# Reordering the first loads of a two-layer decoder trunk: x's first block in two halves, the first weights on ACT's queue, g's row alone

## The chip, the cores and the metric

The kernel runs on one core of a Trainium2 chip. The metric is the device time of one execution, in microseconds; the median of three runs stands for a kernel. The core has five engines that run side by side, each working through its own instructions in the order of the program: TensorE (PE, with its weight loads listed as PEld), VectorE (DVE), ScalarE (ACT), GpSimd (POOL) and SyncE (SP). They wait for one another through semaphores. Transfers are issued from the queues of SP, ACT and POOL.

## The reference

Two layers of a hybrid decoder on x of 512 tokens by 1024 channels, in float32. What matters here is the start of the first layer:

```
def hybrid_layer(x, positions, norm_g, w_in, ...):
    h = rmsnorm(x, norm_g)
    p = h @ w_in                       # (512 x 1024) @ (1024 x 3488)
    (cq, ckv, kr, g_a, ...) = jnp.split(p, offs, axis=-1)
    q = (rmsnorm(cq, mla_q_norm_g) @ mla_w_uq)...
    ...                                # rope(q, positions), attention, conv, gating, block-sparse attention
    return y @ w_out
```

rope needs the cosine and sine of positions times a fixed row of frequencies; positions are integers, one for each token.

## The kernel before

All matrix products split each float32 operand into a high and a low part and add three products (high by high, low weights by high, high by low). The order of all instructions is set at build time by a small planner: class `Order` keeps a model clock for each engine and a heap of generators; each generator is a chain of work that yields until its model time is due, and an instruction is put down when the planner reaches it. The planner moves instructions only between places in the build; on the chip each engine runs its list from the first to the last.

The start goes like this. `start` (L2068) issues the load of the first block of x (128 channels, k = 0, all 512 tokens) on SP, then puts down six matmuls on a tile of ones (`o.fill`, tile `warm`), whose results nobody reads. One more small matmul at L2082 turns 12 rows of the tile `junk` into 12 columns of PSUM: four rows of positions (cast from integers to floats by POOL at L539) and eight rows of the gain g of the first RMSNorm (`norm_g`). DVE copies them to the tile `pg`, whose two parts are called `posf` and `gcol`. The two rows were loaded by two issues on ACT's queue (L537, L538).

`c_first` (L1761) is the first piece of the projection, 416 columns wide, with four accumulators `cq` for the four groups of 128 tokens. It starts with `x_transpose(0)` (L749): four transposes on PE of x's first block into tile `xT`. Then ACT writes the high part `hTh`, scaled by `gcol`, and DVE the low part `hTl`. For each k the three groups of four matmuls follow: `whi` by `hTh`, then the next block's four transposes, `wlo` by `hTh`, `whi` by `hTl`.

The weights of `c_first` come in units `c0` to `c3`, two blocks of k in each. `load_units` (L408) loads unit c0 in two halves on SP and puts the load of x's second block (`load_xk(1, 2)`) between them; `split_units` (L446) makes the high part of each half, by DVE for the first half of c0 and by ACT for the others of c0 to c3, and `low_half` the low part by DVE.

POOL meanwhile fills masks and constants, clears the tile `prow` and issues six small loads of gains into it (`load_rows`, L616 to L623). The rope tables (`rope_tables`, L551, tile `rope_scratch`) come next on POOL and need `posf`. From there on, PE is the engine that everything is arranged around, to the last matmul.

Of the kernel before, what the change touches and what calls it, by code (L numbers as in the profile page):

```python
# [13 lines left out]
I32 = mybir.dt.int32  # L14
AF = mybir.ActivationFunctionType
# [3 lines left out]
P = 128  # L19
S = 512  # L20
NT = S // P
D = 1024
KT = D // P
# [35 lines left out]
def dram(ap, offset, pattern):  # L59
    return bass.AP(tensor=ap.tensor, offset=ap.offset + offset, ap=pattern)  # L60
# [91 lines left out]
def run_now(gen):  # L152

    try:
        next(gen)
    except StopIteration as e:
        return [e.value]
# [64 lines left out]
def hybrid_trunk(ctx: ExitStack, tc: tile.TileContext, x, positions, norm_g, w_c, w_f, w_t, w_o, mla_q_norm_g,  # L222
                 mla_w_uq, mla_kv_norm_g, mla_w_ukv, mla_q_g, mla_k_nope_g, mla_k_rope_g, conv_w,
                 sg_ln_g, sg_ln_b, sg_w, sg_b, moba_q_g, moba_k_g, out):
    nc = tc.nc
    V, A, G, PE = nc.vector, nc.scalar, nc.gpsimd, nc.tensor
# [16 lines left out]
    o = Order()  # L243
# [46 lines left out]
            yield from ch.wait(low)  # L290
        yield from ch.pe(c, PE.matmul, dst, sl, mh, start=False, stop=last, **k)

    def dma(ch, nbytes, dst, src):

        o.clk["D"] = max(o.clk["D"], ch.t) + nbytes / 360.0
        nc.sync.dma_start(dst, src)
        ch.t = o.clk["D"] + 2000.0

    x1d = dr.tile([S, D], F32, name="x1d")
# [108 lines left out]
    def load_units():  # L408
        for u in order:
            ch = Chain(o)  # L410
            u.raw_slots = rawS
            if u.name in ("uq_0", "ukv_0"):
                u.raw_slots = hS
                u.raw = yield from hS.get(ch, f"raw_{u.name}")
            elif u.name[:-3] in SPROD and u.name[-3] == "1":
                u.raw_slots = hS
                u.raw = yield from hS.get(ch, f"raw_{u.name}")
            elif u.name in ("sq2_0", "sq3_0"):
                u.raw_slots = v4S
                u.raw = yield from v4S.get(ch, f"raw_{u.name}", [P, D], F32)  # L420
            elif u.name in ("c2_0", "c3_0") or u.name[:-3] in ZPROD and u.name[-3] == "1":
                u.raw_slots = tkS
                u.raw = (yield from tkS.get(ch, f"raw_{u.name}", 96)).rearrange("p a b c -> p (a b c)")
            else:
                u.raw = yield from rawS.get(ch, u.name)
            key = (int(u.name[-1]), u.name[:-3], ord(u.name[-3]) - 48)
            if key in tsum_ev:
                yield from ch.wait(tsum_ev[key])
            n = u.a * u.b
            if u.name == "c0_0":  # L430
                for i in range(2):
                    sl = slice(i * n // 2, (i + 1) * n // 2)
                    ch = Chain(o)
                    dma(ch, P * n * 2, u.raw[:, sl], u.src[:, sl])
                    o.set(u.landed[i], ch.t)
                    if i == 0:
                        load_xk(1, 2)
            else:
                dma(ch, P * n * 4, u.raw[:, :n], u.src)
                ch.t += LATE.get(u.name, 0.0)  # L440
            o.set(u.loaded, ch.t)
            for e in LOAD_HOOKS.pop(u.name, ()):
                e()
            yield o.now

    def split_units(i0, i1):  # L446
        for u in order[i0:i1]:
            ch = Chain(o)
            if u.name != "c0_0":
                yield from ch.wait(u.loaded)  # L450
            u.hi, u.lo = yield from u.slots.get(ch, u.name)
            n = u.a * u.b
            gain = {"uq": 2 * int(u.name[-1]), "ukv": 4 + int(u.name[-1])}.get(u.name[:-2])
            if gain is not None:
                yield from ch.wait(pc_ev)
            for i in range(2):
                if u.name == "c0_0":
                    yield from ch.wait(u.landed[i])
                while ch.t > o.now + SLACK:
                    yield ch.t - SLACK  # L460
                while not u.wanted and max(o.clk["A"], o.clk["V"]) > o.now + WSLACK:
                    yield o.now + 100.0
                sl = slice(i * n // 2, (i + 1) * n // 2)
                c2 = Chain(o, max(o.now, ch.t))
                hi, lo, raw = u.hi[:, sl], u.lo[:, sl], u.raw[:, sl]
                g = None
                if gain is not None:
                    c = gain + (i if u.a == 2 else 0)
                    g = pcol[:, c:c + 1]
                if o.clk["V"] + 900.0 < o.clk["A"] and u.idx > 3 or u.idx == 0 and i == 0:  # L470
                    if g is None:
                        yield from c2.dve_fast(V.tensor_copy, hi, raw)
                    else:
                        yield from c2.dve(V.tensor_scalar, hi, raw, g, None, op0=ALU.mult)
                else:
                    yield from c2.act(A.activation, hi, raw, AF.Copy, scale=1.0 if g is None else g)
                o.set(u.high[i], c2.t)
                o.spawn(low_half(u, i, c2, lo, raw, hi, g), None, LOPRIO if u.idx < 4 else 5)
                ch.t = max(ch.t, c2.t - LAT)
# [54 lines left out]
    pg = cst.tile([P, NT + KT], F32, name="pg")  # L534
    posf, gcol = pg[:, 0:NT], pg[:, NT:]
    inv = cst.tile([P, 16], F32, name="inv")
    nc.scalar.dma_start(junk[0:NT, 0:P].bitcast(I32), dram(positions, 0, [[P, NT], [1, P]]))  # L537
    nc.scalar.dma_start(junk[NT:NT + KT, P:2 * P], dram(norm_g, 0, [[P, KT], [1, P]]))  # L538
    G.tensor_copy(junk[0:NT, P:2 * P], junk[0:NT, 0:P].bitcast(I32))  # L539
    for i in range(16):  # L540
        G.memset(inv[:, i:i + 1], THETA ** (-i * 2.0 / 32))
    one_box = run_now(zzS.get(Chain(o), "ones", F32R))
# [68 lines left out]

    pcol = cst.tile([P, 14], F32, name="pcol")
    pc_ev = Event()
    prow = []

    def load_rows():  # L616
        pr = prow[0]
# [123 lines left out]
    def load_xk(k0, k1):  # L741
        ch = Chain(o)
        c0 = (k0 % 2) * P
        src = x[0, :, k0 * P:k1 * P].rearrange("(t p) c -> p t c", p=P)
        dma(ch, P * NT * P * 4 * (k1 - k0), xk[k0 // 2][:, :, c0:c0 + (k1 - k0) * P], src)
        for k in range(k0, k1):
            o.set(xk_ev[k], ch.t)

# [995 lines left out]
    def main():  # L1744
# [16 lines left out]
        def c_first(L):  # L1761

            home = [accS, accS, accS, sS]
            a, us = [], {}
            for t in range(NT):
                a.append((yield from home[t].get(m, f"cq{t}_0")))

            def part(k, t, i):
                (hh, hl), (wh, wl) = hk(L, k), us[k]
                sl = slice(t * P, (t + 1) * P)  # L1770
                yield from m.pe(cost(416), PE.matmul, a[t][:, 0:416], (hl if i == 2 else hh)[:, sl],
                                wl if i == 1 else wh, start=k == 0 and i == 0, stop=k == KT - 1 and i == 2)

            def ready(k, i):
                u = units[f"c{k // 2}_0"]
                for v in order[u.idx:u.idx + AHEAD]:
                    v.wanted = True
                yield from m.wait((xhi[k], u.half[k % 2], xlo[k])[i])
                if i == 0:
                    yield from m.wait(u.high[k % 2])  # L1780
                    us[k] = [z[:, k % 2, :] for z in u.view()]

            yield from x_transpose(0)
            for k in range(KSPLIT):
                for i in range(3):
                    yield from ready(k, i)
                    for t in range(NT):
                        yield from part(k, t, i)
                    if i == 0 or i == 1 and k + 1 == KSPLIT:
                        yield from x_transpose(k + 1 + i)  # L1790
                    yield o.now
                if k % 2 == 1:
                    done_unit(f"c{k // 2}_0")
            for t, k in ((0, 6), (1, 6), (0, 7), (1, 7), (2, 6), (2, 7), (3, 6), (3, 7)):
                for i in range(3):
                    if t == 0:
                        yield from ready(k, i)
                    yield from part(k, t, i)
                yield o.now
                if k == KT - 1:  # L1800
                    o.spawn(low_chain(L, t, a[t], o.now + PELAT, home[t]))
            for k in range(KSPLIT // 2, KT // 2):
                done_unit(f"c{k}_0")
# [264 lines left out]
    def start():  # L2068
        o.clk["D"] = 1000.0
        cw = Chain(o)  # L2070
# [4 lines left out]
        ones = one_box[0][:, 0:P].bitcast(F32)  # L2075
        V.memset(ones, 1.0)
        V.tensor_copy(one_box[0][:, P:2 * P], ones)
        A.activation(xsum[:, 0, 0:1], ones[:, 0:1], AF.Square, scale=D ** -0.5)
        o.fill = lambda: PE.matmul(wp[:, 0:P], ones, ones, start=True, stop=True)
        for _ in range(NWARM):  # L2080
            o.fill()
        PE.transpose(wp[:, 256:256 + NT + KT], junk[0:NT + KT, P:2 * P], ident[0:NT + KT, 0:NT + KT])  # L2082
        V.tensor_copy(pg, wp[:, 256:256 + NT + KT])
        o.pe_end, o.fill_until = 3700.0, FILLEND
        o.clk["V"] = 3700.0

# [6 lines left out]
        LOAD_HOOKS["c0_0"] = (lambda: load_xk(2, 4),)  # L2093
        LOAD_HOOKS["c1_0"] = (lambda: load_xk(4, 6),)
        LOAD_HOOKS["c2_0"] = (lambda: load_xk(6, 8),)
        prow.append((yield from t2S.get(cw, "prow")))
        G.memset(prow[0][0:14, 0:P], 1.0)
        load_rows()
        o.clk["G"] = 10000.0
# [65 lines left out]
```

## Time and profile before

| what | value |
|---|---|
| median of three runs | 486.28 us (484.81 to 486.62) |
| profiled execution, span from first to last instruction | 484.2 us |
| profiled execution, time outside its span | not listed; the three runs lie 0.6 to 2.4 us above the span |
| PE busy | 478.2 us, 99% of the span |
| DVE, ACT, POOL busy | 399.4, 335.0, 115.2 us |
| first matmul of the projection (`cq`) starts at | 5.77 us |
| last matmul ends at about | 480.3 us |

The span is the time from the first to the last instruction of one profiled execution. A busy time adds the spans of an engine's instructions. Matmul ends are modelled, so consecutive matmuls overlap in the listing, and the distance of their starts is the better measure of pace.

### The profile page before, as it was taken

The page shows a single profiled execution, that of the slowest core. Times are in us where ns is not written, and L with a number is a line of the kernel's source. Part 1 is how long each engine was busy: PE and PEld are TensorE (multiplying, and loading weights), DVE is VectorE, ACT ScalarE, POOL GpSimd, SP SyncE. Part 2 cuts the span into 40 slices and gives each one's busy share as a digit, 9 for nine tenths or more (in the row PEclk, how much of TensorE's full clock was granted, in tenths as well). Part 3 has the DMA queues.
Part 4 walks back from the last instruction along what each step waited for, and adds up shares of the span by engine and source line. Part 5 has one row for each costly group of instructions (what it writes and reads, how often), then busy time and mean ns, then how long its engine had stood idle before and what let it go on. Part 6 is the DMA issues. An engine that isn't in the chain of part 4 may idle for free. (4 is left out here: it accounts for less than half of the span.)

```text
span 484.2 us, 7554 instructions
## 1 busy us (share of the span) xinstructions
PE 478.2 (99%) x2418; PEld 406.6 (84%) x2418; DVE 399.4 (82%) x883; ACT 335.0 (69%) x895; POOL 115.2 (24%) x187
## 2 busy tenths in 40 slices
PE   8999999999999999999999999999999999999996
PEld 7988888888888888888899888888888888888785
DVE  3698877978798997779898679997788998888992
ACT  5897757776568674457577788788686888676640
POOL 8858713310421052000031004262102200000000
PEclk9999999999999999999999999999999999999999
DMA  8823076996698798685663277987824852248762
GB/s 265 306 87 110 12 229 242 235 232 168 184 282 190 219 270 260 233 283 178 214 238 131 86 268 244 263 176 226 185 87 144 161 156 106 104 158 276 271 216 87
DMA packets 41760, 94.21 MB, mean 195 GB/s; under 512 B 6114, under 2 KB 22328, under 8 KB 41336
## 3 DMA queue, kind: packets, MB, share of 16 engines
q1 hardware_dynamic: 28400, 80.74, 48.2%
q0 software_dynamic: 13216, 12.91, 17.6%
q8 instruction: 19, 0.31, 0.3%
q14 instruction: 21, 0.17, 0.1%
q10 hardware_dynamic: 104, 0.07, 0.1%
HBM read 85.58 MB, written 33.29 MB: 246 GB/s over the span
## 5 line engine op out<-in xcount | busy, mean ns | idle before, releaser
L179 ACT ACTIVATE pd<-pd,mnd 128x128 f32<-128x128 f32 (+3 forms) x53 | 27.2, 541 | 3.7 <-DVE mnd L179 3.5
L179 ACT ACTIVATE pa<-pa,mna 128x128 f32<-128x128 f32 (+3 forms) x55 | 28.1, 539 | 1.8 <-DVE mna L179 1.6
L375 POOL DMA_DIRECT2D t<-in_w_o_dram x16 | 18.6, 1323 | 30.5 <-DMA t<-t 30.4
L179 ACT ACTIVATE pha<-pTa 128x512 fp32r<-128x512 f32 (+3 forms) x32 | 13.8, 436 | 15.1 <-PE pTa L209 14.5
L179 ACT ACTIVATE phd<-pTd 128x512 fp32r<-128x512 f32 (+3 forms) x32 | 13.7, 433 | 13.0 <-PE pTd L209 12.8
L209 PE MATMUL cq<-whi_c,hTh 128*128 128x416 f32 x64 | 20.6, 367 | 0.4 <-ACT hTh L179 0.3
L179 DVE TENSOR_TENSOR pla<-pTa,pha 128x512 fp32r<-128x512 f32 (+3 forms) x32 | 15.1, 485 | 7.1 <-ACT pha L179 7.0
L179 ACT ACTIVATE whi_t<-raw_t 128x512 fp32r<-128x512 f32 x32 | 18.5, 618 | 3.3 <-DMA raw_t<-t 3.3
L179 DVE CUSTOM_DVE_ANT_0 pa<-sa,maskb,rs_q 128x512 f32<-128x512 f32 (+3 forms) x32 | 16.6, 545 | 4.8 <-PE pTa L209 2.7
L179 DVE TENSOR_TENSOR wlo_t<-raw_t,whi_t 128x512 fp32r<-128x512 f32 x32 | 20.6, 680 | 0.0
L209 PE MATMUL cq<-wlo_c,hTh 128*128 128x416 f32 x64 | 20.0, 358 | 0.0
L209 PE MATMUL cq<-whi_c,hTl 128*128 128x416 f32 x64 | 19.8, 356 | 0.0
L179 DVE TENSOR_TENSOR wlo_p<-raw_p,whi_p 128x512 fp32r<-128x512 f32 x28 | 18.9, 698 | 0.7 <-ACT whi_p L179 0.6
L179 DVE TENSOR_TENSOR pld<-pTd,phd 128x512 fp32r<-128x512 f32 (+3 forms) x32 | 15.1, 486 | 4.6 <-ACT phd L179 4.3
L179 DVE CUSTOM_DVE_ANT_0 pd<-sd,maskb,rs_mq 128x512 f32<-128x512 f32 (+3 forms) x32 | 16.7, 545 | 1.6 <-PE pTd L209 0.8
L179 ACT ACTIVATE whi_b<-raw_b 128x512 fp32r<-128x512 f32 x23 | 13.8, 621 | 4.1 <-DMA raw_b<-in_w_o_dram 4.0
L179 DVE TENSOR_TENSOR wlo_b<-raw_b,whi_b 128x512 fp32r<-128x512 f32 x24 | 16.1, 683 | 0.1
L179 ACT ACTIVATE whi_p<-raw_p 128x512 fp32r<-128x512 f32 x26 | 15.6, 625 | 0.7 <-DMA raw_p<-p 0.7
L179 POOL TENSOR_TENSOR rs_mk<-rs_mk,nhalf 128x16 f32<-128x16 f32 x2 | 5.9, 2926 | 42.5 <-ACT gc L179 21.5
L179 POOL TENSOR_SCALAR xss<-xss 128x1 f32<-128x1 f32 x4 | 2.7, 669 | 54.6 <-ACT jk L179 50.2
L375 POOL DMA_DIRECT2D p<-in_w_t_dram x8 | 9.8, 1486 | 23.0 <-DMA p<-p 11.8
L209 PE MATMUL pTa<-ident,pa 128*128 128x128 f32 x80 | 14.0, 273 | 0.0
(499 smaller groups left out, 1854.4 us busy)
## 6 DMA issues: line engine op xcount, KB each, us to landing
t<-in_w_o_dram POOLq DMA_DIRECT2D x16, 512.0 KB, 8.6
raw_t<-t SPq DMA_DIRECT2D x16, 512.0 KB, 4.9
raw_b<-in_w_o_dram SPq DMA_DIRECT2D x12, 512.0 KB, 5.0
t<-in_w_o_dram SPq DMA_DIRECT2D x8, 512.0 KB, 5.3
p<-in_w_t_dram POOLq DMA_DIRECT2D x8, 512.0 KB, 12.4
t<-t SPq DMA_DIRECT2D x8, 512.0 KB, 4.9
raw_p<-p SPq DMA_DIRECT2D x8, 512.0 KB, 4.7
ys<-ysc SPq DMA_DIRECT2D x14, 256.0 KB, 5.6
```

The source lines that it names most:

```text
L179: f(*a, **k)
L209: f(*a, **k)
L375: nc.gpsimd.dma_start(src(l, n, j), src(l, y, j), accum_op=ALU.add, max_dma_last_dim=1024)
```

## The change

The change touches only the start of the program.

- x's first block is loaded by two issues on SP, tokens 0 to 255 and 256 to 511, each with its own semaphore.
- The first half of weight unit c0 is issued by ACT's queue instead of SP's.
- g's eight rows are the first issue on ACT's queue, and the small matmul (now L2092) and the copy behind it (L2093) handle g alone.
- The positions are the third issue on ACT's queue (`begin_act`, called in `load_units` when the first half of c0 has been issued); they land in free columns of `prow`, and POOL's cast of them stands in `begin_act`.
- `pos_cols` puts a second small matmul for the positions behind `x_transpose(0)` (L2096), and DVE copies its result to `posf` a little later (L2100).
- The high part of c0's second half is made by DVE instead of ACT.

```diff
@@ load_units
-                    dma(ch, P * n * 2, u.raw[:, sl], u.src[:, sl])
+                    dma(ch, P * n * 2, u.raw[:, sl], u.src[:, sl], nc.scalar if i == 0 else None)
                     o.set(u.landed[i], ch.t)
                     if i == 0:
+                        o.begin_act()
                         load_xk(1, 2)
@@ split_units
-                if o.clk["V"] + 900.0 < o.clk["A"] and u.idx > 3 or u.idx == 0 and i == 0:
+                if o.clk["V"] + 900.0 < o.clk["A"] and u.idx > 3 or u.idx == 0:
@@ setup
-    nc.scalar.dma_start(junk[0:NT, 0:P].bitcast(I32), dram(positions, 0, [[P, NT], [1, P]]))
-    nc.scalar.dma_start(junk[NT:NT + KT, P:2 * P], dram(norm_g, 0, [[P, KT], [1, P]]))
-    G.tensor_copy(junk[0:NT, P:2 * P], junk[0:NT, 0:P].bitcast(I32))
+    prow = run_now(t2S.get(Chain(o), "prow"))
+    prows = prow[0][0:NT, P:3 * P]
+    nc.scalar.dma_start(junk[0:KT, 0:P], dram(norm_g, 0, [[P, KT], [1, P]]))
@@ load_xk
+        if k0 == 0:
+            nc.sync.dma_start(dst[:, 0:2, :], src[:, 0:2, :])
+            dst, src = dst[:, 2:4, :], src[:, 2:4, :]
+        dma(ch, P * NT * P * 4 * (k1 - k0), dst, src)
@@ c_first
             yield from x_transpose(0)
+            o.pos_cols()
@@ start
-        A.activation(xsum[:, 0, 0:1], ones[:, 0:1], AF.Square, scale=D ** -0.5)
+
+        def begin_act():
+            nc.scalar.dma_start(prows[:, 0:P].bitcast(I32), dram(positions, 0, [[P, NT], [1, P]]))
+            A.activation(xsum[:, 0, 0:1], ones[:, 0:1], AF.Square, scale=D ** -0.5)
+            G.tensor_copy(prows[:, P:2 * P], prows[:, 0:P].bitcast(I32))
+        o.begin_act = begin_act
...
-        PE.transpose(wp[:, 256:256 + NT + KT], junk[0:NT + KT, P:2 * P], ident[0:NT + KT, 0:NT + KT])
-        V.tensor_copy(pg, wp[:, 256:256 + NT + KT])
+        PE.transpose(wp[:, 256:256 + KT], junk[0:KT, 0:P], ident[0:KT, 0:KT])
+        V.tensor_copy(gcol, wp[:, 256:256 + KT])
+
+        def pos_cols():
+            PE.transpose(wp[:, 384:384 + NT], prows[:, P:2 * P], ident[0:NT, 0:NT])
+
+            def take():
+                V.tensor_copy(posf, wp[:, 384:384 + NT])
...
+            o.spawn(take(), 6200.0, -9)
```

Behind these places the order of every engine is the same as before to the end of the program.

The first place is PE's list at the start, from the fill matmuls to the first matmuls of the projection. Before:

```order
L2079 MATMUL warm<-ones 128x128 x6
L2082 MATMUL warm<-ident,junk 128x12
L209 MATMUL xT_224<-ident,x_0_174 128x128 x4
L2079 MATMUL warm<-ones 128x128 x2
L209 MATMUL cq_0_220<-whi_c_0_199,hTh_0_230 128x416
```

Now, where the words in brackets are the semaphores that a row waits for (DVE's, POOL's, ACT's and those of loads):

```order
L2089 MATMUL warm<-ones 128x128 [waits DVE_49]
L2092 MATMUL warm<-ident,junk 128x8 [waits DMAHW0_49,Pool_49]
L209 MATMUL xT_225<-ident,x_0_173 128x128 [waits DMAHW1_49]
L209 MATMUL xT_225<-ident,x_0_173 128x128 [waits DMAHW3_49]
L2096 MATMUL warm<-ident,prow 128x4 [waits DVE_49,Pool_49]
L2089 MATMUL warm<-ones 128x128 x2
L209 MATMUL cq_0_221<-whi_c_0_197,hTh_0_232 128x416 [waits DVE_49,Activation_49]
```

The matmul for the positions, which was part of L2082, now stands as L2096 between the transposes of x's first block and the first `cq` matmul, with a wait for POOL of its own.

The second place is POOL's list, from the last mask to the first row of the rope tables. Before (the constants between L541 and L2097 left out):

```order
L529 AFFINE_SELECT maskb<-maskb 128x128
L539 CAST junk<-junk 4x128
L541 MEMSET inv 128x1 x16
...
L2097 MEMSET prow 14x128
L618 DMA prow<-in_mla_q_norm_g_dram 4x128
L619 DMA prow<-in_mla_kv_norm_g_dram 2x128
L621 DMA prow<-in_mla_q_g_dram 2x2x64
L621 DMA prow<-in_mla_k_nope_g_dram 2x2x64
L623 DMA prow<-in_moba_q_g_dram 2x2x48
L623 DMA prow<-in_moba_k_g_dram 2x2x48
L179 TENSOR_SCALAR rope_scratch<-inv,pg 128x16 x4
```

Now:

```order
L530 AFFINE_SELECT maskb<-maskb 128x128
L542 MEMSET inv 128x1 x16
...
L2117 MEMSET prow 14x128
L618 DMA prow<-in_mla_q_norm_g_dram 4x128
L619 DMA prow<-in_mla_kv_norm_g_dram 2x128
L621 DMA prow<-in_mla_q_g_dram 2x2x64
L621 DMA prow<-in_mla_k_nope_g_dram 2x2x64
L623 DMA prow<-in_moba_q_g_dram 2x2x48
L623 DMA prow<-in_moba_k_g_dram 2x2x48
L2087 CAST prow<-prow 4x128
L179 TENSOR_SCALAR rope_scratch<-inv,pg 128x16 x4
```

The cast of the positions has moved from ahead of the constants to behind the six load issues of POOL.

The third place is DVE's list around the first two weight halves. Before:

```order
L2083 COPY pg<-warm 128x12
L179 CAST whi_c_0_199<-raw_c_0_201 128x416
L179 TENSOR_TENSOR wlo_c_0_200<-raw_c_0_201,whi_c_0_199 128x416
L179 SCALAR_TENSOR_TENSOR hTl_0_231<-xT_224,pg,hTh_0_230 128x512
L179 SCALAR_TENSOR_TENSOR hTl_0_231<-xT_243,pg,hTh_0_230 128x512
```

Now:

```order
L2093 COPY pg<-warm 128x8
L179 CAST whi_c_0_197<-raw_c_0_199 128x416
L179 TENSOR_TENSOR wlo_c_0_198<-raw_c_0_199,whi_c_0_197 128x416
L179 SCALAR_TENSOR_TENSOR hTl_0_233<-xT_225,pg,hTh_0_232 128x512
L179 CAST whi_c_0_197<-raw_c_0_199 128x416
L2100 COPY pg<-warm 128x4
L179 SCALAR_TENSOR_TENSOR hTl_0_233<-xT_245,pg,hTh_0_232 128x512
```

A second cast and the copy of the positions have been put between the low part of x's first block and the low parts that follow.

## Rows read from the trace of the kernel before

**Rows 1.** The page, part 1: busy time, share of the span, instructions of each engine.

```profile
PE 478.2 (99%) x2418; PEld 406.6 (84%) x2418; DVE 399.4 (82%) x883; ACT 335.0 (69%) x895; POOL 115.2 (24%) x187
```

**Rows 2.** Busy time of each engine in stretches of the span.

```profile
core 0: us, PE busy (x) PEld busy (x) DVE busy (x) ACT busy (x) POOL busy (x), PEclk, DMA share, GB/s
0.00:5.77 5.77, 4.16 (x21) 3.68 (x21) 1.46 (x6) 2.17 (x3) 3.91 (x44) 1.00 0.62 167
5.77:30.00 24.23, 24.12 (x137) 22.17 (x138) 16.71 (x34) 20.77 (x65) 19.70 (x45) 1.00 0.72 246
...
60.00:480.00 420.00, 419.56 (x2122) 355.39 (x2121) 354.48 (x773) 288.16 (x735) 70.52 (x72) 1.00 0.69 201
```

**Rows 3.** Timeline of PE at the start: start, duration, instruction, idle before and its releaser.

```profile
1.11 2.93 PE L2079 MATMUL warm<-ones 128*128 128x128 f32 x12 [1.11 <-DVE ones L2076]
...
4.21 0.20 PE L2082 MATMUL warm<-ident,junk 12*128 12x12 f32 x1 [0.17 <-DMA junk<-in_norm_g_dram]
...
4.34 0.65 PE L209 MATMUL xT<-ident,x 128*128 128x128 f32 x4
...
4.83 0.61 PE L2079 MATMUL warm<-ones 128*128 128x128 f32 x4
...
5.77 1.02 PE L209 MATMUL cq<-whi_c,hTh 128*128 128x416 f32 x4 [0.33 <-ACT hTh L179]
...
7.82 0.92 PE L209 MATMUL cq<-whi_c,hTl 128*128 128x416 f32 x4
...
8.84 1.02 PE L209 MATMUL cq<-whi_c,hTh 128*128 128x416 f32 x4
...
10.89 0.92 PE L209 MATMUL cq<-whi_c,hTl 128*128 128x416 f32 x4
...
11.65 0.99 PE L209 MATMUL cq<-whi_c,hTh 128*128 128x416 f32 x4
```

**Rows 4.** The same timeline, POOL from its last mask to the rope tables.

```profile
2.02 0.29 POOL L529 TENSOR_SCALAR_AFFINE_SELECT maskb<-maskb 128x128 f32<-128x128 f32 x1
...
3.12 0.28 POOL L539 CAST junk<-junk 4x128 f32<-4x128 int32 x1 [0.81 <-DMA junk<-in_positions_dram]
3.35 0.58 POOL L541 MEMSET inv<- 128x1 f32 x16
...
4.38 0.20 POOL L2097 MEMSET prow<- 14x128 f32 x1
...
4.88 0.70 POOL L618 DMA_DIRECT2D prow<-in_mla_q_norm_g_dram  x1 [0.31 <-POOL prow L2097]
...
7.85 0.55 POOL L623 DMA_DIRECT2D prow<-in_moba_k_g_dram  x1
...
8.43 1.24 POOL L179 TENSOR_SCALAR rope_scratch<-inv,pg 128x16 f32<-128x16 f32 x4
```

**Rows 5.** The same timeline: ACT, its queue, and DVE's copy of g.

```profile
0.80 0.56 ACTq L537 DMA_DIRECT2D junk<-in_positions_dram  x1
...
4.45 0.17 DVE L2083 COPY pg<-warm 128x12 f32<-128x12 f32 x1 [3.13 <-PE warm L2082]
...
5.03 0.69 ACT L179 ACTIVATE hTh<-xT,pg 128x512 fp32r<-128x512 f32 x1 [1.81 <-PE xT L209]
...
7.26 0.55 ACT L179 ACTIVATE whi_c<-raw_c 128x416 fp32r<-128x416 f32 x1 [0.94 <-DMA raw_c<-in_w_c_dram]
```

**Rows 6.** Waits of PE's weight loads, 5.77 to 60 us: total, times, longest.

```profile
PEld cq L209 <- ACT hTh L179: 1.0, 2, 0.5
PEld cq L209 <- DVE hTl L179: 0.3, 1, 0.3
PEld q L209 <- DVE cTl L179: 0.3, 1, 0.3
PEld pcT L209 <- POOL rope_scratch L179: 0.3, 1, 0.3
```

**Rows 7.** Weight loads of the tile warm: duration min/median/max in ns.

```profile
L2079 PEld LDWEIGHTS warm<-ones x16: 190/333/333, 1.1 to 5.1; 128*128 128x128 f32 x16
```

**Rows 8.** Tile x (its blocks' loads), up to 16 us: time from issue to landing.

```profile
DMA to landing us min/median/max: 3.1/3.9/6.1
```

More of the change, by code (lines that the diff above doesn't have):

```diff
@@ L291, in mm3, with dma @@
         yield from ch.pe(c, PE.matmul, dst, sl, mh, start=False, stop=last, **k)
-    def dma(ch, nbytes, dst, src):
+    def dma(ch, nbytes, dst, src, q=None):
         o.clk["D"] = max(o.clk["D"], ch.t) + nbytes / 360.0
-        nc.sync.dma_start(dst, src)
+        (q or nc.sync).dma_start(dst, src)
         ch.t = o.clk["D"] + 2000.0
@@ L613, in hybrid_trunk @@
     pc_ev = Event()
-    prow = []
     def load_rows():
@@ L744, in load_xk @@
         src = x[0, :, k0 * P:k1 * P].rearrange("(t p) c -> p t c", p=P)
-        dma(ch, P * NT * P * 4 * (k1 - k0), xk[k0 // 2][:, :, c0:c0 + (k1 - k0) * P], src)
+        dst = xk[k0 // 2][:, :, c0:c0 + (k1 - k0) * P]
+        if k0 == 0:
+            nc.sync.dma_start(dst[:, 0:2, :], src[:, 0:2, :])
+            dst, src = dst[:, 2:4, :], src[:, 2:4, :]
+        dma(ch, P * NT * P * 4 * (k1 - k0), dst, src)
         for k in range(k0, k1):
@@ L2081, in start @@
             o.fill()
-        PE.transpose(wp[:, 256:256 + NT + KT], junk[0:NT + KT, P:2 * P], ident[0:NT + KT, 0:NT + KT])
-        V.tensor_copy(pg, wp[:, 256:256 + NT + KT])
+        PE.transpose(wp[:, 256:256 + KT], junk[0:KT, 0:P], ident[0:KT, 0:KT])
[4 more added lines that the diff above has]
+                V.tensor_copy(posf, wp[:, 384:384 + NT])
+                return
+                yield
+            o.spawn(take(), 6200.0, -9)
+        o.pos_cols = pos_cols
         o.pe_end, o.fill_until = 3700.0, FILLEND
@@ L2095, in start @@
         LOAD_HOOKS["c2_0"] = (lambda: load_xk(6, 8),)
-        prow.append((yield from t2S.get(cw, "prow")))
         G.memset(prow[0][0:14, 0:P], 1.0)
```

## The prediction

> **What bounds the kernel now.** I read the page's busy times first. PE is busy for 478.2 of 484.2 us, and no other engine is above 82% [rows 1]. A busy share is an average, so the next view was the stretches: from the first `cq` matmul at 5.77 us to 30 us PE is busy for 24.12 of 24.23 us, and from 60 to 480 us for 419.56 of 420.00 us [rows 2]. So PE, once it has begun with the projection, runs through to the last matmul almost without a stop. What the change can be worth, either way, is therefore the moment at which that stream begins, plus the few waits inside it. It is a question about the first 12 us, and there the timeline has to be read instruction by instruction.
>
> In PE's timeline [rows 3] the reader sees a chain: fill matmuls from 1.11 to 4.04 us, the small matmul of g and positions at 4.21, the four transposes of x's first block from 4.34 to 4.99, two fill matmuls (four records) to 5.44, and the first `cq` group at 5.77. The gap of 0.33 us before 5.77 is a wait for ACT, which makes `hTh` from 5.03 to 5.72 [rows 5]. One more stop is visible by the starts of the groups: from the third group of one block to the first group of the next the step is 11.65 − 10.89 = 0.76 us when nothing is late, and 8.84 − 7.82 = 1.02 us at the second block. That stop of 0.26 us comes from ACT, which waits 0.94 us for the second half of unit c0, converts it from 7.26 to 7.81, and only afterwards makes the second block's `hTh` [rows 5]. These are what the change aims at. Behind them the weight loads of PE show three more waits of 0.3 us each up to 60 us [rows 6].
>
> POOL's timeline matters because a PE instruction waits for it. POOL casts the positions at 3.12, writes constants from 3.35, clears `prow` at 4.38, and from 4.88 issues six loads, each of which occupies POOL for 0.55 to 0.70 us; the last one starts at 7.85 and ends at 8.40, and the rope tables follow at 8.43 [rows 4]. That rope instruction needs only constants and `pg`, which DVE had written by 4.62 us [rows 5]. So it was held by nothing but the six issues: on POOL, what stands behind them waits for all of them.
>
> **The change part by part.** *The positions.* The cast now stands behind the six issues, and PE's matmul of the positions (L2096) waits for it. Behind L2096 on PE stand the two fill matmuls and the whole projection. Before, the cast ended at 3.40 us and PE reached its matmul at 4.21, so nothing was lost; now the cast is late. How late: POOL no longer waits for the positions at 3.12 (0.81 us of idle time) nor casts there, so the constants start when the last mask ends, at about 2.02 + 0.29 = 2.31 instead of 3.35. All that follows moves up by 1.04 us. The last issue then ends at 8.40 − 1.04 = 7.36, the cast takes 0.28 and ends at about 7.65. The positions themselves are the third issue on ACT's queue, about 1.2 us later than before by two issues of 0.56 us or less [rows 5]; before they had landed by 3.12, so they are there by 4.4 or so and bind nothing.
>
> PE then starts L2096 at about 7.70 (`hTh` ends on ACT at 5.72 and PE starts on it at 5.77, so 0.05 us from engine to engine). From the small matmul to the next instruction it was 4.34 − 4.21 = 0.13; then come four fill records, which before took 0.61 us with ends that overlap, so 0.45 to 0.61 of path. I take 0.45, near the lower end, since four transposes of the same width follow one another within 4.83 − 4.34 = 0.49. The first `cq` group starts at 7.72 + 0.13 + 0.45 = 8.30 us instead of 5.77. That is **+2.53 us**. Bounds: if POOL's six issues or the cast run 0.3 us shorter or longer than before, 2.2 to 2.9.
>
> *g alone, x in halves, c0 by ACT's queue.* These can only move what happens before 7.7 us. The last of it was ready on PE's side at 5.72, so they would have to make something 2 us later to matter; x's blocks land 3.1 to 6.1 us after their issue [rows 8], the second half of x's first block is issued some 0.5 us after the first, and no row puts its landing near 7.7. They cost and give nothing; if the stall by POOL weren't there, they would be worth what the third rival says. The loading of ACT's tables, which now starts two issues later, ends before `hTh` is wanted.
>
> *c0's second half by DVE.* At the second block PE would now come 2.5 us later than before, at about 11.3, and `hTh`, which ended at 8.79 before and needs the transposes at about 9.2 to 9.8 now, is written by about 10.5. The stop of 0.26 us goes: **−0.26**. It would go by the delay alone. On DVE the copy of the positions stands between that cast and its low part, and waits for L2096 too, to about 7.95; the low part is then written by about 8.7, before PE asks for it. What waits behind on DVE (`hTl` of the second block) isn't wanted before 12.
>
> *The waits further on.* The 0.3 us at `pcT` stand at the loads of `prow`, which are issued 1.04 us earlier while PE comes 2.3 us later: **−0.2**, between 0 and −0.3. The waits for `hTl` and `cTl` are for DVE, whose work follows PE's own transposes and moves along with them: 0, at best −0.6. Sum: 2.53 − 0.26 − 0.2 = **+2.07 us**, between +1.3 and +2.9. On the span that makes 484.2 + 2.1 = 486.3; on the median of the runs, 2.1 above that span, 486.28 + 2.1 = 488.4 us.
>
> **The clock.** In the listing PEclk reads 1.00 from the start [rows 2], but the weight loads say otherwise: those of the fill tile take 333 ns in the first stretch and 190 ns, as all later ones, after 4.7 us [rows 7]; twelve records take 2.93 us there and four take 0.61 later [rows 3]. So PE begins at the lower level of 1.2 GHz and has the upper one of 2.4 GHz by 4.7 us, after some 3 us of fill work. In the changed kernel PE would have nothing to do from about 4.9 to 7.7 us. No row of before shows a pause of that length in the middle, so whether the clock falls is open. The Trainium skill speaks against the change here (TensorE: Matmul & The Clock Gate, "Why this matters for your kernels"): matmul bursts are to be kept close together, or an idle TensorE is put back to half its clock. By that page the sum would be the one of the first rival; by the rows alone it stays at +2.07.
>
> **The rivals.** *The pause also costs the clock.* L2096 and the projection would begin at 1.2 GHz and stay there about as long as at the start, 2.9 us, with loads of 333 instead of 190 ns: 2.9 × (1 − 190/333) = 1.25 us lost, twice that if it takes twice as long. Time: 488.4 + 1.25 = 489.6 us, up to 490.9. For it: the start of this very trace, which shows the low level after idleness. Against: the pause is about 2.9 us long, and the transposes and fills lie close before it. This one puts the kernel on the slower side of what can be told apart; it decides if the loads of the first `cq` group take more than 300 ns.
>
> *The delay is given back.* While PE waits, ACT, DVE and the loads run ahead, and PE's later waits could vanish. They can't be worth more than they are: rows 6 sum to 1.9 us, so 2.53 − 1.9 = +0.6, 486.9 us. Against it: most of these waits are for engines that follow PE's own results.
>
> *PE is not held.* If the cast came through between the issues, the path would be the shorter start: the fill ends at 4.04 instead of the 4.21 at which g let PE go, x's halves land between 3.9 (0.80 and 3.1 us, as the whole did) and about half a microsecond later, and the stop of 0.26 us goes. That is −0.43 to +0.1, some 486.0 us: not slower, and the change would have done as it says. Against: the rope row at 8.43.
>
> **How the numbers follow.** Held by POOL with the clock kept: 0.52, 488.4 us. With the clock lost: 0.35, 489.6. Given back: 0.08, 486.9. Not held: 0.05, 486.0. The runs of before spread by 1.8 us, so I call 0.5%, 2.43 us, what can just be told from no change; the border lies at 488.71. Of the first case about 0.3 falls above it for the spread of a median and the bounds of the sum, of the second nine tenths: 0.16 + 0.31 = 0.47 slower. Faster by 2.43 us is reached by no case; 0.02 stays for the runs themselves. The rest, 0.51, is within. The range goes from 486.6, which leaves out the cases that give most back, to 490.6, which leaves out a clock that stays low for twice as long. Within the likeliest case alone it would be 487.6 to 489.2.
>
> **What would show it.** Right: POOL's cast L2087 starting at about 7.4 right behind the last L623; L2096 on PE at about 7.7 with a wait for POOL of nearly 3 us; the first `cq` group at about 8.3; no step over 0.8 us at the second block; all later PE work 2.0 to 2.3 us later than before. The clock: weight loads of the first `cq` groups near 188 or near 333 ns. Wrong: a cast before the issues, a first `cq` below 6.5 us, or a stretch from 10 to 60 us in which PE's starts come closer to those of before by more than half a microsecond.

## The result, and the profile after

The changed kernel takes 489.5 us (median of six runs, 488.6 to 491.8) against 485.96 us for the kernel before in its six runs. The ratio is 1.0079, with a 95% interval of 1.0063 to 1.0094. The kernel is slower by 3.5 us by the medians, by 3.8 us by the ratio. The profiled execution has a span of 487.8 us against 484.2.

PE is still busy for 99% of the span; the page's first line looks like that of before [rows 1]:

```profile
PE 480.5 (99%) x2419; PEld 409.5 (84%) x2419; DVE 399.1 (82%) x885; ACT 334.9 (69%) x894; POOL 113.9 (23%) x187
```

So the busy share says nothing. The timeline of PE at the start, to be laid beside [rows 3], does (start, duration, instruction, idle before and its releaser):

```profile
1.12 2.93 PE L2089 MATMUL warm<-ones 128*128 128x128 f32 x12 [1.12 <-DVE ones L2081]
...
3.98 0.27 PE L2092 MATMUL warm<-ident,junk 8*128 8x8 f32 x1
...
4.18 1.47 PE L209 MATMUL xT<-ident,x 128*128 128x128 f32 x4
...
7.87 0.27 PE L2096 MATMUL warm<-ident,prow 4*128 4x4 f32 x1 [2.22 <-POOL prow L2087]
...
8.07 1.22 PE L2089 MATMUL warm<-ones 128*128 128x128 f32 x4
...
8.94 1.73 PE L209 MATMUL cq<-whi_c,hTh 128*128 128x416 f32 x4
```

After the transposes PE stands still until 7.87 us, released by POOL's cast of the positions. The first `cq` group starts at 8.94 us, 3.17 us later than before, and takes 1.73 us where it took 1.02.

POOL in the same timeline, beside [rows 4]:

```profile
2.27 0.60 POOL L542 MEMSET inv<- 128x1 f32 x16
...
3.80 0.70 POOL L618 DMA_DIRECT2D prow<-in_mla_q_norm_g_dram  x1 [0.31 <-POOL prow L2117]
...
6.92 0.62 POOL L623 DMA_DIRECT2D prow<-in_moba_k_g_dram  x1
...
7.54 0.28 POOL L2087 CAST prow<-prow 4x128 f32<-4x128 int32 x1
```

The six issues have moved up by 1.08 us and the cast follows the last of them without a gap. The weight loads of PE show the second half of the loss:

```profile
4.96 0.29 PEld L209 LDWEIGHTS xT<-ident,x 128*128 128x128 f32 x2 [0.49 <-DMA x<-in_x_dram]
...
8.88 1.24 PEld L209 LDWEIGHTS cq<-whi_c,hTh 128*128 128x128 f32 x4
...
12.37 1.23 PEld L209 LDWEIGHTS cq<-whi_c,hTl 128*128 128x128 f32 x4
13.60 0.75 PEld L209 LDWEIGHTS cq<-whi_c,hTh 128*128 128x128 f32 x4
```

Four loads of the projection take 1.24 us until about 13.4 us and 0.75 from there on. The lower of the two clock levels lasts to 13.4 us here; in the kernel before all loads after 4.7 us were at the upper one [rows 7]. The column of the granted clock (PEclk, the last but two) doesn't show this low level: it reads 1.00, as at the start of the kernel before [rows 2], so here the level has to be read from the loads.

```profile
8.90:13.40 4.50, 4.50 (x16) 4.24 (x16) 1.42 (x3) 1.80 (x6) 3.30 (x10) 1.00 1.07 372
```

The first row of the loads above also shows that the transposes waited 0.49 us for the second half of x's first block.

At the second block's first group the delay is 13.79 − 8.84 = 4.95 us. At the end it is 3.6 us, so this execution made up 1.35 us on that of the kernel before. The weight loads' waits after 60 us tell where most of it was. Before:

```profile
PEld ox L209 <- DVE wlo_t L179: 0.6, 1, 0.6
PEld t0a L209 <- ACT mix L179: 0.5, 1, 0.5
PEld sd L209 <- ACT mk0d L179: 0.4, 1, 0.4
PEld od L209 <- DVE pld L179: 0.4, 1, 0.4
PEld od L209 <- ACT phd L179: 0.2, 1, 0.2
```

After, the whole answer for that stretch is one row:

```profile
PEld sd L209 <- ACT mk0d L179: 0.4, 1, 0.4
```

Four of the five waits for other engines are absent here. That PE came later isn't shown to be the reason, as the runs below tell.

### The profile page after: what moved, and what is told of

Read it like the earlier page. It is cut to its first block, busy times and chain, and to the rows that moved or that the text cites. A ratio compares the mean times of both kernels' runs of the same rounds, so it can differ in the third digit from the quotient of the medians.

```text
span 487.8 us, 7558 instructions
## 1 busy us (share of the span) xinstructions
PE 480.5 (99%) x2419; PEld 409.5 (84%) x2419; DVE 399.1 (82%) x885; ACT 334.9 (69%) x894; POOL 113.9 (23%) x187
## 4 chain that ended last, share of the span: by engine, by line
PE 98%; POOL 1%; issue 0%; DVE 0%; POOLq 0%
PE cq L209 8%; PE oy L209 6%; PE kv L209 6%; PE gd L209 5%; PE cb L209 5%; PE gc L209 5%; PE cc L209 5%; PE su L209 5%; PE ch L209 5%; PE gb L209 5%; PE sq L209 4%; PE ox L209 4%; PE ga L209 4%; PE oz L209 4%; PE py L209 3%; PE sa L209 3%
## 5 line engine op out<-in xcount | busy, mean ns | idle before, releaser
L179 POOL TENSOR_TENSOR ms<-ms,nhalf 128x2 f32<-128x2 f32 x8 | 6.8, 856 | 33.0 <-DVE ms L179 33.0
```

The lines of the kernel that those rows point to most:

```text
L179: f(*a, **k)
```

## The experiments

My theory after the result: the pause of PE on POOL's cast is the whole loss, once by its length and once by the time at the low clock that goes with it. The main rival: the new loads (x in halves, the first weights on ACT's queue) make the start late, and the pause only covers that. A second rival: when the clock rises is chance, whatever PE did. Each ratio below is against the kernel before on the same chip (medians 485.6 to 485.7 us).

**POOL's cast ahead of its six issues.** The clearing of `prow` and the six issues are put behind the cast, in `begin_act`:

```diff
             G.tensor_copy(prows[:, P:2 * P], prows[:, 0:P].bitcast(I32))
+            G.memset(prow[0][0:14, 0:P], 1.0)
+            load_rows()
...
-        G.memset(prow[0][0:14, 0:P], 1.0)
-        load_rows()
```

> The changed kernel with one thing altered: POOL's cast of the positions stands ahead of its six load issues. Theory (the pause of PE on POOL's cast, with the time at the low clock that follows from it, is the whole loss): the small matmul of the positions no longer waits, the first cq group starts at about 6.4 us instead of 8.94 (x's second half of tokens landed at 4.96 in the changed kernel, and the chain from there to cq takes 1.4 us), the stop of 0.26 us at the second block stays away; time about 486.4 us against 486.0 of the kernel before and 489.5 of the changed one. Rival (the loads: x in halves and the first weights on ACT's queue make the start late): the time stays at 488.5 or above.

Measured: 486.6 us, ratio 1.0008 (0.9993 to 1.0023). Of the 0.79% at most 0.23% is left, and the interval includes no loss at all. In its timeline POOL casts at 4.87 and PE goes through:

```profile
4.87 0.31 POOL L2087 CAST prow<-prow 4x128 f32<-4x128 int32 x1 [1.52 <-DMA prow<-in_positions_dram]
```

```profile
4.17 1.27 PE L209 MATMUL xT<-ident,x 128*128 128x128 f32 x4
5.38 0.26 PE L2098 MATMUL warm<-ident,prow 4*128 4x4 f32 x1
5.57 1.22 PE L2091 MATMUL warm<-ones 128*128 128x128 f32 x4
6.45 1.73 PE L209 MATMUL cq<-whi_c,hTh 128*128 128x416 f32 x4
```

The first `cq` group starts at 6.45, as the theory had it. It takes 1.73 us, so this execution was still at the low clock there, without any pause.

**The small matmul of the positions late.** `pos_cols` is called behind the first block's three groups:

```diff
             yield from x_transpose(0)
-            o.pos_cols()
...
                         yield from x_transpose(k + 1 + i)
+                    if k == 0 and i == 2:
+                        o.pos_cols()
```

> The changed kernel with POOL's list left as it is, but the small matmul of the positions behind the three groups of the first block on PE instead of ahead of them. Theory: PE has nothing of POOL's to wait for at 5.7 us, first cq at about 6.4 us, the small matmul reached at about 9 us, when the cast has long ended at 7.8; time about 486.4 us, like the version with the cast ahead of the issues. Rival (the loads make the start late): 488.5 or above.

Measured: 486.3 us, ratio 1.0013 (0.9999 to 1.0026). POOL is as late as in the changed kernel, but nobody waits for it: in PE's timeline the small matmul at 8.99 has no wait, and `cq` starts at 6.09.

```profile
6.09 1.02 PE L209 MATMUL cq<-whi_c,hTh 128*128 128x416 f32 x4 [0.33 <-ACT hTh L179]
...
8.99 0.22 PE L2097 MATMUL warm<-ident,prow 4*128 4x4 f32 x1
```

**Work for PE in the pause.** Five fill matmuls ahead of the small one:

```diff
             yield from x_transpose(0)
+            for _ in range(5):
+                o.fill()
             o.pos_cols()
```

> The changed kernel with five more fill matmuls on PE right ahead of the small matmul of the positions, so that PE works during part of the pause (from 5.65 to about 7.8 us). Nothing that the projection needs moves. Theory that the pause costs twice (its own length, and a clock that rises late because PE did nothing): the weight loads of the first cq groups take 188 instead of 333 ns, the first cq group starts no later than 8.94, and the time falls by about 1.3 us to 488.2. Rival (when the clock rises is chance, whatever PE did): no change, 489.5, or 489.9 if the fill itself delays the small matmul.

Measured: 488.25 us, ratio 1.0050 (1.0032 to 1.0068), against 1.0079 (1.0063 to 1.0094) of the changed kernel. In PE's timeline the pause is filled, the small matmul waits only 0.44 us, and the first `cq` group starts at 8.31 at the upper clock:

```profile
5.47 1.77 PE L2091 MATMUL warm<-ones 128*128 128x128 f32 x10
7.69 0.23 PE L2098 MATMUL warm<-ident,prow 4*128 4x4 f32 x1 [0.44 <-POOL prow L2089]
7.84 0.71 PE L2091 MATMUL warm<-ones 128*128 128x128 f32 x4
8.31 1.00 PE L209 MATMUL cq<-whi_c,hTh 128*128 128x416 f32 x4
```

Useless work in front of a wait made the kernel faster, though the two intervals overlap a little (1.0063 to 1.0068). The difference of the ratios is 0.29%, 1.4 us; the medians, each against its own kernel before, differ by 0.9 us (3.5 and 2.6). Adding the two half-widths as squares, I estimate that the 0.29% lies between 0.05% and 0.53%. Read as the price of the clock it is small and poorly known; the delay alone is the 0.50% that stays, 2.4 us.

**The split of g and positions alone.** x whole, c0 on SP's queue, the second half's high part by ACT (`load_xk`, `load_units` and `split_units` as before); the rest as changed.

> The kernel before with the split of g and positions alone: x's first block in one load, both halves of the first weights on SP's queue and the second half's high part by ACT as before, but the cast of the positions behind POOL's six issues and their matmul ahead of the first cq group. Theory (the pause on POOL's cast is the whole loss): first cq at about 8.3 to 8.9 us and a time of 489.0 to 489.5, as in the changed kernel. Rival (the loads make the start late): 486.5 or below.

Measured: 489.4 us, ratio 1.0069 (1.0052 to 1.0087). This part of the change alone gives the loss. Its weight loads and stretches show the clock falling behind the pause:

```profile
7.62 0.14 PEld L2093 LDWEIGHTS warm<-ident,prow 4*128 4x128 f32 x1 [2.74 <-POOL prow L2084]
...
8.21 0.68 PEld L209 LDWEIGHTS cq<-whi_c,hTh 128*128 128x128 f32 x4
...
9.81 1.24 PEld L209 LDWEIGHTS cq<-wlo_c,hTh 128*128 128x128 f32 x4
```

```profile
5.60:8.90 3.30, 1.28 (x9) 1.26 (x10) 1.42 (x4) 1.78 (x6) 2.08 (x6) 1.00 1.03 317
9.00:12.30 3.30, 3.30 (x13) 3.08 (x12) 0.95 (x2) 2.00 (x7) 2.88 (x9) 0.50 1.07 376
```

The first `cq` loads are fast (0.68 us for four), those from 9 us on slow; the granted clock in the last column but two is 1.00 to 8.9 us and 0.50 from 9.0 to 12.3. PE had then been at work again for 1.3 us, since 7.62.

One profile can't tell how often the clock falls so, but the mean granted clock of every single execution was recorded. It is 0.996, 0.995 and 0.995 in three of the six executions of the changed kernel, and 0.995, 0.996 and 0.995 in three of the six of the split alone. The profile above has 0.996, so such a value is a stay of this kind at half the clock. In none of the 183 executions of the other kernels is it below 0.997, and in the six with the fill it is 0.998 to 1.000. So the unfilled pause brings the granted clock down in half of the executions, and no kernel without it shows such a value. The profiled execution of the changed kernel is one of the other half (1.000): it shows no upper level before 13.4 us that could have fallen. The executions with a recorded fall are no slower than that other half (488.1 to 489.7 us against 489.3 to 491.8), so a mean near 1 is no sign of a fast start either.

The theory stands on four legs: take the wait away in two ways and the loss goes, make it alone and the loss comes, fill it and the falls of the clock go, with about a microsecond of the time.

**Which of the load edits does what.** The next three start from the kernel with the small matmul late. They undo x's halves, c0 on ACT's queue, and both. First x whole:

```diff
-        if k0 == 0:
-            nc.sync.dma_start(dst[:, 0:2, :], src[:, 0:2, :])
-            dst, src = dst[:, 2:4, :], src[:, 2:4, :]
```

> The changed kernel with the small matmul of the positions behind the first block's groups (no pause), and x's first block loaded in one issue again; the first half of c0 stays on ACT's queue. Theory (x in halves, its second half issued half a microsecond later and sharing the transfer engines with c0, is what eats the gain of the other edits: x's second half let PE go at 4.76 to 4.96 us, the whole at 4.17 or earlier): the transposes run without a wait from about 4.17, first cq at about 5.4 to 5.7 us instead of 6.09 to 6.45; time about 485.2, 0.5 to 0.8 us below the version with the halves. Rival (c0 on ACT's queue is what delays x, halves or not): the transposes still wait to 4.6 or later, first cq at 6.0 or later, no gain over the version with the halves.

Measured: 485.5 us, ratio 1.0001 (0.9990 to 1.0012). Then c0's first half back on SP's queue, x in halves:

```diff
-                    dma(ch, P * n * 2, u.raw[:, sl], u.src[:, sl], nc.scalar if i == 0 else None)
+                    dma(ch, P * n * 2, u.raw[:, sl], u.src[:, sl])
```

> The changed kernel with the small matmul of the positions late, x's first block in two halves, and the first half of c0 on SP's queue behind them. Theory (the halves eat the gain): x's second half is still later than the whole, the weights of c0 come half a microsecond later too, first cq at 5.8 to 6.3 us, time about 485.8 to 486.3, no better than with c0 on ACT's queue. Rival (c0 on ACT's queue is what delays x): the transposes no longer wait beyond 4.3, first cq at about 5.4 us, time about 485.2.

Measured: 486.2 us, ratio 1.0009 (0.9996 to 1.0023). Then both:

> Small matmul of the positions late, x's first block whole, c0's first half on SP's queue: of the change only g's row first and alone and c0's second half by DVE are left. Theory: the transposes start at about 4.0 to 4.17 us (g is no longer waited for at 4.21), first cq at about 5.4 to 5.6 us, no stop of 0.26 us at the second block: about 485.1 us, 0.5 below the kernel before. Rival (the start is set by the clock's rise and not by these edits): 485.6 within 0.2.

Measured: 485.6 us, ratio 0.9999 (0.9990 to 1.0008). The times of these three, and of the version with both edits in, cannot be told apart by their intervals. Their profiles can be read, though. With x in halves and c0 on ACT's queue the transposes waited 0.29 to 0.52 us for x in all four profiles that have it; in these three they don't wait, each profile showing the same row but for its last digits, here the one with x whole:

```profile
4.18 1.11 PE L209 MATMUL xT<-ident,x 128*128 128x128 f32 x4
```

So it takes both edits for x to be late, and neither of my two theories (the halves, or ACT's queue) is right by itself. With x whole and c0 on ACT's queue it is c0 that is late: DVE's first cast waits for it until 5.55 us, which doesn't delay the first `cq`, since ACT's `hTh` is not done before 6.02 either. In all three the transposes ran at the low clock (1.11 us where the kernel before has 0.65), and `cq` started at 6.07, not at the 5.4 to 5.6 that I expected: the rival of the last run, that the clock's rise sets the start, fits. In fact the kernel before's profile is the only one of the twelve in which all four transposes ran at the upper level. The next kernel, which was profiled twice and has the kernel before's PE list, starts `cq` at 6.01 and 6.21, so that 5.77 was on the early side.

**c0's second half by DVE alone**, on the kernel before:

```diff
-                if o.clk["V"] + 900.0 < o.clk["A"] and u.idx > 3 or u.idx == 0 and i == 0:
+                if o.clk["V"] + 900.0 < o.clk["A"] and u.idx > 3 or u.idx == 0:
```

> The kernel before with one edit: the high part of c0's second half by DVE. Theory: first cq at 5.77 us as before, ACT makes the second block's high part of x as soon as its transposes are done, so the stop of 0.26 us at the second block goes and time falls by 0.26 us to about 485.4, less than 5 rounds can tell apart. Rival (DVE becomes late instead, since its low part of the second half stands behind the cast): the stop stays or grows, 485.6 to 485.9.

Measured: 485.2 us, ratio 0.9989 (0.9973 to 1.0005). The stop at the second block is gone by the timeline, 9.11 − 8.36 = 0.75 us:

```profile
6.01 1.02 PE L209 MATMUL cq<-whi_c,hTh 128*128 128x416 f32 x4 [0.33 <-ACT hTh L179]
7.10 0.66 PE L209 MATMUL xT<-ident,x 128*128 128x128 f32 x4
7.52 1.00 PE L209 MATMUL cq<-wlo_c,hTh 128*128 128x416 f32 x4
8.36 0.92 PE L209 MATMUL cq<-whi_c,hTl 128*128 128x416 f32 x4
9.11 0.92 PE L209 MATMUL cq<-whi_c,hTh 128*128 128x416 f32 x4
```

In that execution the next block's transposes then came 0.23 us late, 1.09 us after the first `cq` start instead of 0.86. Since the interval reached across 1, the same kernel ran again beside one that also issues g ahead of the positions on ACT's queue (the two `dma_start` lines of L537 and L538 exchanged).

> The same kernel as the one with DVE's high part alone, a second time, beside the kernel before on this chip, since the first time left 0.9989 with an interval across 1. Theory: ratio 0.9990 to 0.9995 (0.26 us of 485.65). Rival (nothing gained): 1.000 within 0.0005.

> The kernel before with c0's second half's high part by DVE, and the two issues on ACT's queue in the other order (g first, positions second); one small matmul for both, as before. Theory: the stop at the second block goes (0.26 us) and PE no longer waits for g behind the fill (0.1 to 0.2 us): 485.2 to 485.3 against 485.65, ratio 0.9990. Rival (when the clock rises sets the start, and the edits are lost in it): ratio 1.000 within 0.001.

Measured: 0.9999 (0.9988 to 1.0011) for the repeat, 0.9997 (0.9987 to 1.0006) with g first. The two values of the same kernel lie on both sides of the 0.26 us that it should gain; a quarter of a microsecond stays below what these runs can show. Nor is the stop simply gone: in the repeat's profile the step at the second block is 9.02 − 8.26 = 0.76 us, but PE waits for ACT's `hTh` again at the third and the fourth block, where the kernel before had no such wait:

```profile
11.93 0.68 PEld L209 LDWEIGHTS cq<-whi_c,hTh 128*128 128x128 f32 x4 [0.39 <-ACT hTh L179]
...
15.01 0.68 PEld L209 LDWEIGHTS cq<-whi_c,hTh 128*128 128x128 f32 x4 [0.45 <-ACT hTh L179]
```

No version was measurably faster than the kernel before.

## Why the prediction was right or wrong

The measured 489.5 us lies in the range, and the direction and the mechanism, PE held by a cast behind POOL's six issues, were right. The likeliest case was not the one that came: I put 0.52 on a kept clock and 488.4 us, and 0.35 on the clock as the first rival, 489.6 us. That the rival's number is met to 0.1 us is luck: two of its terms were off by more than a microsecond each and cancel, as the paragraphs on the clock and on the waits show. One bound was also added up wrongly: the lower ends of my terms give 2.2 − 0.26 − 0.3 − 0.6 = +1.0 and the upper ends +2.6, not +1.3 and +2.9.

*The positions, and POOL's six issues.* Right. I had the cast starting at 7.36 and the small matmul at 7.70; they came at 7.54 and 7.87, because POOL's six issues took 0.2 us longer in all than before (3.80 to 7.54 us, against 4.88 to 8.40). In the kernel with the fill, where the issues took as long as before, the small matmul came at 7.69 and `cq` at 8.31 against my 7.70 and 8.30. The positions themselves landed later than the 4.4 that I had: where POOL waits for them it casts at 4.87. That bound nothing in the changed kernel.

*The clock.* I chose the wrong case, and the price that I gave the other was too small for the execution that was profiled. The first `cq` group came at 8.94 instead of 8.30: 0.17 us of this are POOL's, the rest is the fill behind the small matmul, which ran at the low clock too. The projection stayed there to 13.4 us. At the second block's first group the changed kernel is 13.79 − 11.10 = 2.69 us behind the run with the fill; 0.18 of that is the small matmul (7.87 against 7.69), so the low level cost 2.5 us up to there, twice the 1.25 that I had priced. It lasted 5.3 us of work (8.07 to 13.4) where I had 2.9. My bound for twice the time covered this, but it was not in the 489.6.

I had described the rival as a clock that falls in the pause. By the granted clocks that happened in three of the six executions; in the profiled one no row before 13.4 shows the upper level at all. The page that I had cited against the change (the Trainium skill, TensorE: Matmul & The Clock Gate, "Why this matters for your kernels": an idle engine is put back to half its clock) describes the fall, and the run with the split alone agrees with its 0.50. That the clock rises at different moments stands in the same page of the Trainium skill, Part 1, which calls the number of slow matmuls run-variable; the traces agree: the first `cq` group took 1.73 us from 6.45 in one execution without a pause, and 1.02 us from 6.09 in another.

*g alone, x in halves, c0 by ACT's queue.* Right that they cost nothing under the stall. Too kind where I priced the start without it: I had −0.43 to +0.1 us for the case that PE is not held, and the two kernels that show it have ratios of 1.0008 and 1.0013, 0.4 and 0.6 us above, though both intervals include 1. x's second half did not land half a microsecond after the whole's 3.9 us but let PE go at 4.76 to 4.99. The Trainium skill (DMA: Bandwidth & Descriptors, "Issuing engines are not separate DMA queues") says that issues from several engines run on the same transfer engines and interleave, which saves only issue time. The traces agree in part: with c0 issued from ACT's queue beside it, x's second half held the transposes to 4.76 us or later in four profiles of four, and with c0 behind it on SP's queue it didn't in the one profile that shows it. c0 itself is not seen to come later by it: DVE's first cast of c0 starts at 4.63 to 4.81 us in those four, and at 4.53 to 4.97 in the six with x whole and both loads on SP's queue.

*c0's second half by DVE.* The stop of 0.26 us went, as computed: 11.10 − 10.35 = 0.75 us between the groups in the run with the fill, and 0.75 with this edit alone. I had not counted that ACT can be late at the blocks behind it, as the repeat shows.

*The waits further on.* Mis-sized: I took 0.2 us and read the waits up to 60 us only. The profiled execution made up 1.35 us from the second block to the end, most of it after 60 us, where the weight loads' waits were 0.4 us in total and not 2.1. With the low clock's 2.5 us this closes the sum: 2.53 + 0.17 + 2.5 − 0.26 − 1.35 = 3.6 us. But the rival that the delay is given back is not borne out by it. With the small matmul late, where `cq` starts only 0.3 us later than before, the same single wait of 0.4 us is left after 60 us. In the run with the fill, where PE is 2.3 us late, there are more of these waits than in the kernel before, and the 2.69 us between it and the changed kernel shrink to the 1.0 us between the two spans:

```profile
PEld oy L209 <- DVE wlo_t L179: 0.9, 2, 0.7
PEld ox L209 <- DVE wlo_t L179: 0.5, 1, 0.5
PEld sd L209 <- ACT mk0d L179: 0.4, 1, 0.4
PEld od L209 <- DVE pld L179: 0.4, 1, 0.4
PEld od L209 <- ACT phd L179: 0.4, 1, 0.4
```

Over the twelve profiles the waits for DVE and ACT after 60 us add up to between 0.4 and 2.6 us, in no order with PE's start. The kernel before's profile, from which I worked, was at the high end. What makes them long or short stays open.

## What to carry to other kernels

An instruction that is moved takes the queue of its new place with it: a 0.28 us cast behind six load issues of POOL kept the engine that bounds the kernel idle for 2.2 us, because one small matmul waited for it in front of everything. Before moving work to a "later" place, list what stands ahead of it on its own engine and what stands behind its consumer on the other one. Where a wait of the bounding engine can't be avoided early in a kernel, useless matmuls in it are worth a try: here they saved about 1 us, which six runs on each side could only just tell from nothing. And the waits in a single profile are a sample: a second profile of the same kernel would have kept me from building on its 5.77 and its late waits.

## What the runs showed of the hardware

The moment at which TensorE comes to the upper clock differed widely between profiled executions whose PE lists are the same up to the transposes. From the length of four weight loads (0.68 us or 1.24) it lies before 6 us in the run with the small matmul late and beyond 8.6 us in the one with the cast ahead, which had worked on PE almost without a gap since 1.1 us. At the second block's first group, with the same PE work behind them, the two stand at 9.14 and 10.75 us. The start thus carries a spread of over 1 us that no edit of the order explains, and single profiles of such variants can't be compared by when `cq` starts. What decides the moment stays open; it wasn't tried. A fall is recorded as well: after PE had stood idle for 2.3 us, from 5.3 to 7.6, the granted clock went to 0.50 at about 9.0 us and stayed there to about 12.3, and a mean granted clock of 0.995 or 0.996 marks six of the twelve executions with such a pause and none of the others.
